# Attention steps in one hand-kept order: a second buffer for compressed scores, small work in other places of six steps, outputs split in mid-step, weights split later

## The chip, the cores and the metric

The kernel runs on one core of a Trainium2 chip. The metric is the device time of one execution in microseconds (us); of several executions the median is given. The engines are named as the profile names them: PE (TensorE, with its weight loads as PEld), DVE (VectorE), ACT (ScalarE), POOL (GpSimd) and SP (SyncE, which here only issues DMAs). Each engine works through its own instructions strictly in order; an instruction whose semaphore has not come holds up everything behind it on that engine.

## What is computed

Two decoder layers on one sequence of 512 tokens of width 1024: a convolution module with a feed-forward net, then native sparse attention with a feed-forward net. Only the attention matters here. Cut to that:

```python
def nsa_attention(h, positions, w_in, q_gain, k_gain, cmp_pos, cmp_w1, cmp_b1, cmp_w2, w_out):
    # 16 heads of 64, 4 key/value groups, three branches: compressed, selected, window
    proj = h @ w_in                       # q, 6 x k/v, gates
    ...
    s_c = einsum(q, k_cmp) * scale        # 31 compressed keys of one group
    p_c = masked_softmax(s_c, cmp_end <= t)
    o_c = einsum(p_c, v_cmp)
    ...                                   # all 8 blocks are within the top 16, so
    p_s = masked_softmax(einsum(q, k_s) * scale, tok <= t)     # causal over 512 keys
    o_s = einsum(p_s, v_s)
    p_w = masked_softmax(einsum(q, k_w) * scale, mask_w)       # a window of 512: causal too
    o_w = einsum(p_w, v_w)
    o = g[0] * o_c + g[1] * o_s + g[2] * o_w
    return o @ w_out
```

## The kernel before

Everything is kept transposed: features on the 128 partitions, the 512 tokens along the free axis. A matrix in fp32 is split into a high part (rounded to fp32r) and the rest, so a product is two or three matmuls; the splits are an ACT copy for the high part and a DVE subtraction for the low part.

Heads are worked two at a time. A *tile* `j` (0 to 7) holds two heads; a *pair* `p` (0 to 3) holds tiles `2p` and `2p+1`. A *unit* is one tile in one branch, selected (`br` 1) or window (`br` 2), so there are 16 units, in the order of `us`. The loop at the end of `nsa` runs steps `n` = 1 to 17: step `n` makes the scores of unit `n`, transposes the probabilities of unit `n-1` and multiplies them with the values; the last product of unit `n-2` falls at the head of the step. Unit 0's scores are made ahead of the loop.

In the loop the order on every engine is as the code is written (`fixed[0] = hold[0] = True`; `kept`, `pe` and `keep_in_program_order` mark the instructions). Outside the loop, and for DMA issues without such a mark, a planner with its own cost model sets the order. One step does this:

- `sc_(par, t)`: scores of 128 queries against up to 512 keys for one head (`L1746`, `L1747`: two matmuls into a PSUM tile `S`, of which there are three), then on DVE the mask and the row maximum (`L1749`, into `Pm`), then on ACT the exponential with its row sum (`L1750`).
- `weigh_(par, t)`: DVE reciprocal of two row sums (`L1760`), then POOL scales two blocks of `Pm` by it and by the gate (`L1764`).
- `flip_`: four PE transposes of `Pm` (`L1777`) into a PSUM tile `T`, copied out as `t` by ACT (`L1782`, tags `t2`, `t0`) or by DVE (`L1780`, tag `t1`).
- `values`: the products with the values into the PSUM tile `O` (`L1803`); for `br` 1 they begin with the compressed branch's product, `pch`, `pcl` with `vch`, `vcl` (`L1795` to `L1797`).
- `o_split`: when a tile's `O` is complete (at the head of steps 3, 5, ... 17), ACT copies the high part `oh` (`L1815`) and DVE subtracts for `ol` (`L1816`). It stands just ahead of slot d.
- four *slots* "a" to "d", at fixed places in the step, where `slot(z)` runs the small work that `q_pair` put into `work[n, z]`.

The small work of a pair is its query tiles and its compressed branch: `move` (four DMAs from SP, which make two stacked copies `q2` of a query tile; three buffers), `stack_hi` (the high part `St`, one copy on POOL `L1499` and one on ACT `L1501`), `stack_lo` (DVE subtraction on 64 partitions, `L1507`), `scores` (eight small matmuls into the PSUM tile `psc`, `L1513`), `masked` (DVE, `psc` into the SBUF tile `sc`, `L1518`; it reads and writes one half of `sc` for each tile of the pair), `top` (`L1528`), `minus` (`L1531`), `exps` (ACT, `L1534`), `valid` (POOL, `L1537`), `sums` (four DVE instructions, `L1543` to `L1549`), `weighed` (POOL, `L1552`), `trans` (four PE transposes of `sc` into the PSUM tile `pct`, `L1557`) and `parts` (ACT `pch` `L1564`, DVE `pcl` `L1565`). Pair 0 does this ahead of the loop, but for `trans` and `parts` (`qp0[4]`, step 1). `sc` has one buffer, so the first `masked` of a pair waits for the `trans` of the pair before.

PSUM has eight banks: three for `S`, two for `O`, and three (tag `p2`) that `T`, `psc` and `pct` share. A tile of tag `p2` gets the bank that the planner expects to be free first.

`W_AT` names the steps at whose end the first two weight tiles of the output projection are split (`w_hi` on ACT, `L219`; `w_lo` on DVE, `L228`); the projection (`proj_tile`, `L279` to `L281`) follows the loop.

Of the kernel before, what the change touches and what calls it, by code (L numbers as in the profile page):

```python
# [19 lines left out]
P = 128  # L20
T = 512
# [99 lines left out]
def trunk(ctx: ExitStack, tc: tile.TileContext, A, out):  # L121
    nc = tc.nc
# [1076 lines left out]
    def nsa(acc, gnext):  # L1199
# [3 lines left out]
        for i in range(2):  # L1203
            t = rp.tile([P, T], F32, name=f"tab{i}")
# [13 lines left out]
        def consts(p):  # L1218
            z = qk.tile([P, T], F32, tag="q2", name="cn", bufs=Q2B)
            nc.sync.dma_start(z[:, :256], A["cn"][:, N_VM:N_VM + 256])  # L1220
            ez = [qk.tile([64, T], F32, tag=t, name=nm("cne"), bufs=b) for t, b in (("q2", Q2B), ("sc", 1))]
            for i in range(2):
                nc.sync.dma_start(ez[i][:, :384], A["cn"][:64, N_E + 384 * i:N_E + 384 * i + 384])
            sel = p.tile([P, 76], F32, name="sel")
            nc.sync.dma_start(sel, A["cn"][:, N_SEL:N_E])
            nc.sync.dma_start(mask[:, 384:], A["cn"][:, N_MASK:N_MASK + 128])
            er = p.tile([P, 6, P], F32R, name="er")
            nc.gpsimd.memset(er[64:].bitcast(F32), 0.0)

# [245 lines left out]
        def kept(z):  # L1475
            return tc.keep_in_program_order(z) if fixed[0] else z

        def q_pair(p):

            a = p // 2  # L1480
            sc = qk.tile([P, 4, 2, 64], F32, tag="sc", name=nm("sc"), bufs=1)

            def move(jj):
                q = oT[2 * p + jj]
                box["q2", jj] = []
                for par in range(2):
                    hs = slice(par * 64, par * 64 + 64)
                    q2 = qk.tile([P, T], F32, tag="q2", name=nm("q2"), bufs=Q2B)
                    for half in range(2):
                        nc.sync.dma_start(q2[half * 64:half * 64 + 64], q[hs])  # L1490
                    box["q2", jj].append(q2)

            def stack_hi(jj):
                S2 = qk.tile([P, 1088], F32R, tag="S", name=nm("St"), bufs=3)
                for par in range(2):
                    q2 = box["q2", jj][par]
                    S = S2[:, par * T:par * T + T]
                    if p > 0 and par in STK_P:
                        kept(nc.gpsimd.tensor_copy(S, q2))  # L1499
                    else:  # L1500
                        kept(nc.scalar.activation(S, q2, AF.Copy))  # L1501
                    qst[2 * p + jj, par] = S

            def stack_lo(jj, par):
                ls = slice(64 - par * 64, 128 - par * 64)
                S, q2 = qst[2 * p + jj, par], box["q2", jj][par]
                kept(nc.vector.tensor_tensor(S[ls], q2[ls], S[ls], ALU.subtract))  # L1507
# [9 lines left out]
            def masked(jj):  # L1517
                kept(nc.vector.scalar_tensor_tensor(  # L1518
                    sc[:, :, jj, :], box["psc", jj], -1.0,
                    cc[:, C_CADD:C_CADD + 256].rearrange("p (t n) -> p t n", t=4), ALU.mult, ALU.add))  # L1520
# [33 lines left out]
            def trans():  # L1554
                pt = box["pct"] = p2.tile([P, T], F32, tag="p2", name=nm("pct"))
                for t in range(4):
                    tc.keep_in_program_order(nc.tensor.transpose(  # L1557
                        pt[:, t * P:(t + 1) * P], sc[:, t].rearrange("p j n -> p (j n)"), ident))

            def parts():  # L1560
                pt = box["pct"]
                ph = q3[1].tile([P, T], F32R, tag="pch", name=nm("pch"))
                pl = q3[1].tile([P, T], F32R, tag="pcl", name=nm("pcl"))
                kept(nc.scalar.activation(ph, pt, AF.Copy))  # L1564
                kept(nc.vector.tensor_tensor(pl, pt, ph, ALU.subtract))  # L1565
                pcT[p] = (ph, pl)
# [6 lines left out]
            if p == 0:  # L1573
                return [lambda: (move(0), scores(0), masked(0)), lambda: (both(0), scores(1), masked(1)),
                        lambda: (move(1), top(), minus(), exps()), lambda: (both(1), valid(), sums(), weighed()),
                        lambda: (trans(), parts())]
            n = max(1, 4 * p - 4)
            jobs = {
                (n, "a"): [lambda: move(0)],
                (n, "c"): [lambda: scores(0)],  # L1580
                (n, "d"): [lambda: masked(0), lambda: stack_hi(0)],
                (n + 1, "a"): [lambda: stack_lo(0, 0)],
                (n + 1, "c"): [lambda: scores(1)],
                (n + 1, "d"): [lambda: masked(1), lambda: stack_lo(0, 1), lambda: move(1)],
                (n + 2, "a"): [top],
                (n + 2, "d"): [minus, exps, lambda: stack_hi(1)],
                (n + 3, "a"): [valid, lambda: stack_lo(1, 0)],
                (n + 3, "d"): [sums, weighed],
                (n + 4, "a"): [lambda: stack_lo(1, 1), trans],
                (n + 4, "b"): [parts],  # L1590
            }
            for z, fs in jobs.items():
                work.setdefault(z, []).extend(fs)

# [77 lines left out]
        qp0 = []  # L1672
# [111 lines left out]
        ob = {}  # L1784
# [22 lines left out]

        split_o = []

        def o_split():  # L1810
            while split_o:
                o = ob[split_o.pop()]
                h_ = op.tile([P, T], F32R, tag=f"o{len(oh)}", name=nm("oh"))
                l_ = oha.tile([P, T], F32R, name=nm("ol"))
                kept(nc.scalar.activation(h_, o, AF.Copy))  # L1815
                kept(nc.vector.tensor_tensor(l_, o, h_, ALU.subtract))  # L1816
                oh.append(h_)
                ol.append(l_)

        us = [(j, br) for j in range(8) for br in (1, 2)]  # L1820
# [23 lines left out]
        for n in range(1, N + 2):  # L1844
            S = n < N
            F = n <= N
            if S:
                start(n)

            def sc_(par, *ts):  # L1850
                if S:
                    for t in ts:
                        score(U[n][par], t)

            def weigh_(par, t):
# [12 lines left out]
            flip_("t2", nc.scalar, (0, 2), (1, 2))
            if n > 1:
                values(U.pop(n - 2), (0,))  # L1870
            slot("a")
            weigh_(0, 2)
            sc_(0, 1, 0)
            slot("b")
            flip_("t1", nc.vector, (0, 1), (0, 3))
            sc_(1, 3)
            weigh_(0, 0)
            flip_("t1", nc.vector, (1, 1), (1, 3))
            sc_(1, 2)
            slot("c")  # L1880
            if n == 1:
                qp0[4]()
            flip_("t0", nc.scalar, (0, 0))
            sc_(1, 1, 0)
            weigh_(1, 2)
            flip_("t0", nc.scalar, (1, 0))
            o_split()
            slot("d")
            weigh_(1, 0)
            if n in W_AT:  # L1890
                w_hi(state["next"] + W_AT.index(n))
                w_lo(state["next"] + W_AT.index(n))
            if F:
                values(U[n - 1], (3, 2, 1))
        assert not work, work
        o_split()
        fixed[0] = hold[0] = False
        sx.close()
        ax.close()
# [179 lines left out]
```

## Time and profile before

| | |
|---|---|
| median of 3 runs | 1237.39 us (1235.42 to 1237.41) |
| the profiled execution | 1237.64 us, of which the span from first to last instruction is 1235.9 us |
| mean granted TensorE clock | 0.996 |
| PE busy over the span | 97% |
| steps 1 to 15 of the loop | 688.56 to 835.97 us: 147.41 us |
| step 16 and 17, to the first matmul of the output projection | 835.97 to 842.46 us: 6.49 us |

A step is counted here from its first score matmul (`L1746` with 512 columns, head 0) to that of the next. A row of the view by windows gives a stretch, its length, the busy time of PE, PEld, DVE, ACT and POOL in it with the number of instructions, the clock that TensorE was granted (1.00 is full), the busy share of the DMA engines and their rate. A row of the timeline gives the start, the length, the engine, the line, the operation, the tiles it writes and reads, its shape, and in brackets how long the engine had been idle and what ended that. A row of the view of waits gives who waited for whom, the sum, how often, and the longest.

### The profile page before, as it was taken

The page shows a single profiled execution, that of the slowest core. Times are in us where ns is not written, and L with a number is a line of the kernel's source. Part 1 is how long each engine was busy: PE and PEld are TensorE (multiplying, and loading weights), DVE is VectorE, ACT ScalarE, POOL GpSimd, SP SyncE. Part 2 cuts the span into 40 slices and gives each one's busy share as a digit, 9 for nine tenths or more (in the row PEclk, how much of TensorE's full clock was granted, in tenths as well). Part 3 has the DMA queues.
Part 4 walks back from the last instruction along what each step waited for, and adds up shares of the span by engine and source line. Part 5 has one row for each costly group of instructions (what it writes and reads, how often), then busy time and mean ns, then how long its engine had stood idle before and what let it go on. Part 6 is the DMA issues. An engine that isn't in the chain of part 4 may idle for free.

```text
span 1235.9 us, 22090 instructions
## 1 busy us (share of the span) xinstructions
PE 1199.9 (97%) x8519; PEld 1042.9 (84%) x8519; DVE 900.8 (73%) x1722; ACT 604.2 (49%) x1116; POOL 245.3 (20%) x349
## 2 busy tenths in 40 slices
PE   9999999999999999999998989989999999999998
PEld 6788688799999989887777766667778999998998
DVE  6996598877777576866697767763597777766775
ACT  5221464455555444543444667773354555554443
POOL 2011002011111102202332556652000111110120
PEclk9999999999999999999999999999999999999999
DMA  8748628277777667554265011015323877774882
GB/s 303 266 129 300 173 85 238 86 180 185 183 186 176 156 192 157 110 182 114 61 146 154 18 27 27 9 35 154 103 85 114 194 183 187 186 175 120 226 164 92
DMA packets 88378, 181.11 MB, mean 147 GB/s; under 512 B 36816, under 2 KB 38480, under 8 KB 86736
## 3 DMA queue, kind: packets, MB, share of 16 engines
q1 hardware_dynamic: 66816, 109.99, 29.2%
q0 software_dynamic: 21456, 69.71, 24.7%
q8 instruction: 67, 1.10, 0.4%
q14 instruction: 39, 0.32, 0.1%
HBM read 165.60 MB, written 5.80 MB: 139 GB/s over the span
## 4 chain that ended last, share of the span: by engine, by line
PE 79%; DVE 9%; ACT 4%; issue 3%; SPq 2%; DMA 2%; POOL 1%; DVEq 0%; ACTq 0%; POOLq 0%
PE st L915 27%; PE st L1105 10%; PE pp L279 7%; PE pp L281 7%; PE pp L280 7%; PE st L281 2%; PE st L280 2%; PE st L279 2%; PE cpe L540 2%; PE pv L1639 2%; PE O L1803 2%; ACT Pm L1750 2%; DVE Pm L1749 1%; PE T L1777 1%; DVE wl L228 1%
## 5 line engine op out<-in xcount | busy, mean ns | idle before, releaser
L219 ACT ACTIVATE wh<-wr 128x1024 fp32r<-128x1024 f32 (+4 forms) x150 | 152.9, 1019 | 201.8 <-PE pp L280 67.7
L228 DVE TENSOR_TENSOR wl<-wr,wh 128x1024 fp32r<-128x1024 f32 (+4 forms) x150 | 180.8, 1205 | 47.8 <-ACT wh L219 47.6
L915 PE MATMUL st<-bh,sl 128*128 128x256 f32 x680 | 192.6, 283 | 1.1 <-DVE sl L899 1.1
L915 PE MATMUL st<-bh,sh 128*128 128x256 f32 x680 | 192.7, 283 | 0.0
L915 PE MATMUL st<-bl,sh 128*128 128x256 f32 x680 | 192.1, 282 | 0.0
L279 PE MATMUL pp<-hh,wh 128*128 128x512 f32 x400 | 159.6, 402 | 2.2 <-ACT wh L219 2.1
L281 PE MATMUL pp<-hh,wl 128*128 128x512 f32 x400 | 157.9, 398 | 1.4 <-DVE wl L228 1.4
L280 PE MATMUL pp<-hl,wh 128*128 128x512 f32 x400 | 158.4, 397 | 0.0
L915 PEld LDWEIGHTS st<-bh,sl 128*128 128x128 f32 x680 | 130.2, 192 | 1.5 <-DVE sl L899 1.5
L915 PEld LDWEIGHTS st<-bl,sh 128*128 128x128 f32 x680 | 130.6, 192 | 0.1
L915 PEld LDWEIGHTS st<-bh,sh 128*128 128x128 f32 x680 | 130.0, 191 | 0.1
L899 DVE TENSOR_TENSOR sl<-S,sh 128x512 fp32r<-128x512 f32 x136 | 87.9, 688 | 51.7 <-ACT sh L898 51.7
L1764 POOL TENSOR_SCALAR Pm<-Pm,sm,gates 128x512 f32<-128x512 f32 (+3 forms) x128 | 81.4, 648 | 70.6 <-DVE sm L1760 63.5
L279 PEld LDWEIGHTS pp<-hh,wh 128*128 128x128 f32 x400 | 75.8, 190 | 23.2 <-ACT wh L219 4.6
L1750 ACT ACTIVATE Pm<-Pm,mx 128x512 f32<-128x512 f32 (+3 forms) x128 | 71.1, 556 | 49.3 <-DVE mx L1749 36.6
L281 PEld LDWEIGHTS pp<-hh,wl 128*128 128x128 f32 x400 | 75.5, 189 | 20.3 <-DVE wl L228 3.1
L280 PEld LDWEIGHTS pp<-hl,wh 128*128 128x128 f32 x400 | 75.8, 190 | 18.0 <-issue 1.1
L1105 PE MATMUL st<-oz,soh 128*128 128x256 f32 x448 | 79.6, 280 | 0.0
L898 ACT ACTIVATE sh<-S 128x512 fp32r<-128x512 f32 x136 | 77.6, 620 | 0.0
L915 PE MATMUL st<-bl,wh 128*128 128x256 f32 x272 | 76.2, 280 | 0.0
L915 PE MATMUL st<-bh,wl 128*128 128x256 f32 x272 | 76.1, 280 | 0.0
L915 PE MATMUL st<-bh,wh 128*128 128x256 f32 x272 | 76.1, 280 | 0.0
(308 smaller groups left out, 2778.8 us busy)
## 6 DMA issues: line engine op xcount, KB each, us to landing
S<-fw_x POOLq DMA_DIRECT2D x68, 512.0 KB, 5.9
wr<-fw_in SPq DMA_DIRECT2D x46, 512.0 KB
So<-fw_q POOLq DMA_DIRECT2D x38, 448.0 KB, 5.8
bd<-bands POOLq DMA_DIRECT2D x12, 1280.0 KB, 11.9
wr<-fw_q SPq DMA_DIRECT2D x24, 448.0 KB
r<-fw_x SPq DMA_DIRECT2D x34, 256.0 KB
wr<-fw_p SPq DMA_DIRECT2D x16, 512.0 KB
wr<-cw_in SPq DMA_DIRECT2D x14, 512.0 KB
```

The lines of the kernel that those rows point to most:

```text
L219: parted(after(nc.scalar.activation(hi[:, :cols], raws[i][:, :cols], AF.Copy), pin.get(AF)))
L228: parted(after(nc.vector.tensor_tensor(lo[:, :cols], raws[i][:, :cols], hi[:, :cols], ALU.subtract), pin.get(ALU)))
L279: held(nc.tensor.matmul(ps, wh, xh, start=first, stop=False))
L280: held(nc.tensor.matmul(ps, wh, xl, start=False, stop=False))
L281: held(nc.tensor.matmul(ps, wl, xh, start=False, stop=last))
L540: last["conv"] = nc.tensor.matmul(ps[e * 64:e * 64 + 16 * m, g, :], w, f[:, g0 + g, 4 - s:68 - s], start=s == 0, stop=s == 4)
L898: pe(nc.scalar.activation(h_[:, c], z, AF.Copy))
L899: pe(nc.vector.tensor_tensor(l_[:, c], z, h_[:, c], ALU.subtract))
L915: pe(nc.tensor.matmul(ps[:, :H], p_[:, k], m_[c][:, t], start=first and c == 0 and q == 0, stop=last and c == 3 and q == 2, skip_group_che ...
L1105: pe(nc.tensor.matmul(ps, a[:, c], b[:, t], start=p in (1, 4) and i == 0 and r == 0, stop=i == NO - 1 and r == 2, skip_group_check=True))
L1750: kept(nc.scalar.activation(Pt, Pt, AF.Exp, bias=mx, scale=-1.0, accum_out=sm))
L1764: kept(nc.gpsimd.tensor_scalar(Pt, Pt, sm[:, k:k + 1], gates[:, t + k, br * 16 + h:br * 16 + h + 1], ALU.mult, ALU.mult))
```

## The change

`sc` gets a second buffer. The two weight tiles are split at the end of steps 14 and 16, not 13 and 14. `o_split` becomes `o_hi`, which stands at the head of slot b's work ahead of the `t1` flips, and `o_lo`, which stands after the last score ahead of slot c. Pair 0's `trans` moves to the front of slot a in step 1, and its `parts` to the place ahead of slot c. Pairs 1 to 3 get new places, spread over six steps:

| small work | pair 1, before | pair 1, after | pairs 2, 3 (`n` = 4, 8), before | pairs 2, 3, after |
|---|---|---|---|---|
| `move(0)` | 1a | 1a | n, a | n+1, d |
| `scores`, `masked` of both tiles | 1c, 1d, 2c, 2d | the same | n and n+1, c and d | the same |
| `stack_hi(0)`, `stack_lo(0, ·)` | 1d; 2a, 2d | the same | n, d; n+1, a and d | n+2, a; n+2, d and n+3, a |
| `top`; `minus`, `exps` | 3a; 3d | 3a | n+2, a; d | n+2, c; d |
| `move(1)` | 2d | 3d | n+1, d | n+3, b |
| `valid`; `sums`, `weighed` | 4a; 4d | 3b; 3d | n+3, a; d | the same |
| `trans`; `parts` | 5a; 5b | 4a; 4c | n+4, a; b | n+4, a; c |
| `stack_hi(1)`, `stack_lo(1, ·)` | 3d; 4a, 5a | 4a; 4d, 5a | n+2, d; n+3, a and n+4, a | n+4, a; n+4, d and n+5, a |

```diff
-W_AT = (13, 14)
+W_AT = (14, 16)
...
-            sc = qk.tile([P, 4, 2, 64], F32, tag="sc", name=nm("sc"), bufs=1)
+            sc = qk.tile([P, 4, 2, 64], F32, tag="sc", name=nm("sc"), bufs=2)
...
-            n = max(1, 4 * p - 4)
+            n = 4 * p - 4
             jobs = {
-                (n, "a"): [lambda: move(0)],
                 (n, "c"): [lambda: scores(0)],
-                (n, "d"): [lambda: masked(0), lambda: stack_hi(0)],
-                (n + 1, "a"): [lambda: stack_lo(0, 0)],
+                (n, "d"): [lambda: masked(0)],
                 (n + 1, "c"): [lambda: scores(1)],
-                (n + 1, "d"): [lambda: masked(1), lambda: stack_lo(0, 1), lambda: move(1)],
-                (n + 2, "a"): [top],
-                (n + 2, "d"): [minus, exps, lambda: stack_hi(1)],
-                (n + 3, "a"): [valid, lambda: stack_lo(1, 0)],
+                (n + 1, "d"): [lambda: masked(1), lambda: move(0)],
+                (n + 2, "a"): [lambda: stack_hi(0)],
+                (n + 2, "c"): [top],
+                (n + 2, "d"): [minus, exps, lambda: stack_lo(0, 0)],
+                (n + 3, "a"): [valid, lambda: stack_lo(0, 1)],
+                (n + 3, "b"): [lambda: move(1)],
                 (n + 3, "d"): [sums, weighed],
-                (n + 4, "a"): [lambda: stack_lo(1, 1), trans],
-                (n + 4, "b"): [parts],
+            } if p > 1 else {
+                (1, "a"): [lambda: move(0)],
+                (1, "c"): [lambda: scores(0)],
+                (1, "d"): [lambda: masked(0), lambda: stack_hi(0)],
+                (2, "a"): [lambda: stack_lo(0, 0)],
+                (2, "c"): [lambda: scores(1)],
+                (2, "d"): [lambda: masked(1), lambda: stack_lo(0, 1)],
+                (3, "a"): [top, minus, exps],
+                (3, "b"): [valid],
+                (3, "d"): [sums, weighed, lambda: move(1)],
             }
+            jobs.update({
+                (n + 4, "a"): [trans, lambda: stack_hi(1)],
+                (n + 4, "c"): [parts],
+                (n + 4, "d"): [lambda: stack_lo(1, 0)],
+                (n + 5, "a"): [lambda: stack_lo(1, 1)],
+            })
...
-        def o_split():
+        def o_hi():
             while split_o:
-                o = ob[split_o.pop()]
-                h_ = op.tile([P, T], F32R, tag=f"o{len(oh)}", name=nm("oh"))
+                j = split_o.pop()
+                h_ = op.tile([P, T], F32R, tag=f"o{j}", name=nm("oh"))
+                kept(nc.scalar.activation(h_, ob[j], AF.Copy))
+                oh.append(h_)
+
+        def o_lo():
+            if len(ol) < len(oh):
                 l_ = oha.tile([P, T], F32R, name=nm("ol"))
-                kept(nc.scalar.activation(h_, o, AF.Copy))
-                kept(nc.vector.tensor_tensor(l_, o, h_, ALU.subtract))
-                oh.append(h_)
+                kept(nc.vector.tensor_tensor(l_, ob[len(ol)], oh[-1], ALU.subtract))
                 ol.append(l_)
...
+            if n == 1:
+                qp0[4]()
             slot("a")
             weigh_(0, 2)
             sc_(0, 1, 0)
             slot("b")
+            o_hi()
             flip_("t1", nc.vector, (0, 1), (0, 3))
             sc_(1, 3)
             weigh_(0, 0)
             flip_("t1", nc.vector, (1, 1), (1, 3))
             sc_(1, 2)
+            o_lo()
+            if n == 1:
+                qp0[5]()
             slot("c")
-            if n == 1:
-                qp0[4]()
             flip_("t0", nc.scalar, (0, 0))
             sc_(1, 1, 0)
             weigh_(1, 2)
             flip_("t0", nc.scalar, (1, 0))
-            o_split()
             slot("d")
             weigh_(1, 0)
```

More of the change, by code (lines that the diff above doesn't have):

```diff
@@ L1220, in consts @@
             nc.sync.dma_start(z[:, :256], A["cn"][:, N_VM:N_VM + 256])
-            ez = [qk.tile([64, T], F32, tag=t, name=nm("cne"), bufs=b) for t, b in (("q2", Q2B), ("sc", 1))]
+            ez = [qk.tile([64, T], F32, tag=t, name=nm("cne"), bufs=b) for t, b in (("q2", Q2B), ("sc", 2))]
             for i in range(2):
@@ L1575, in q_pair @@
                         lambda: (move(1), top(), minus(), exps()), lambda: (both(1), valid(), sums(), weighed()),
-                        lambda: (trans(), parts())]
-            n = max(1, 4 * p - 4)
+                        trans, parts]
+            n = 4 * p - 4
             jobs = {
-                (n, "a"): [lambda: move(0)],
                 (n, "c"): [lambda: scores(0)],
-                (n, "d"): [lambda: masked(0), lambda: stack_hi(0)],
-                (n + 1, "a"): [lambda: stack_lo(0, 0)],
+                (n, "d"): [lambda: masked(0)],
                 (n + 1, "c"): [lambda: scores(1)],
-                (n + 1, "d"): [lambda: masked(1), lambda: stack_lo(0, 1), lambda: move(1)],
-                (n + 2, "a"): [top],
-                (n + 2, "d"): [minus, exps, lambda: stack_hi(1)],
-                (n + 3, "a"): [valid, lambda: stack_lo(1, 0)],
-                (n + 3, "d"): [sums, weighed],
-                (n + 4, "a"): [lambda: stack_lo(1, 1), trans],
-                (n + 4, "b"): [parts],
-            }
+                (n + 1, "d"): [lambda: masked(1), lambda: move(0)],
[4 more added lines that the diff above has]
+                (n + 3, "b"): [lambda: move(1)],
+                (n + 3, "d"): [sums, weighed],
+            } if p > 1 else {
[8 more added lines that the diff above has]
+                (3, "d"): [sums, weighed, lambda: move(1)],
+            }
+            jobs.update({
[4 more added lines that the diff above has]
+            })
             for z, fs in jobs.items():
@@ L1895, in nsa @@
         assert not work, work
-        o_split()
         fixed[0] = hold[0] = False
```

## The prediction

> **What bounds the kernel now.** I read the page's first lines, then the loop cut at its steps (the view by windows: steps 1 to 15, and last the drain), then PE's waits inside the loop, then the timeline at each long wait.
>
> ```profile
> span 1235.9 us, 22090 instructions
> core 0: us, PE busy (x) PEld busy (x) DVE busy (x) ACT busy (x) POOL busy (x), PEclk, DMA share, GB/s
> 688.56:699.61 11.05, 9.21 (x65) 6.95 (x63) 7.22 (x29) 8.34 (x24) 5.17 (x9) 1.00 0.00 0
> 699.61:708.06 8.45, 8.45 (x62) 6.31 (x60) 6.72 (x25) 6.00 (x19) 4.70 (x8) 1.00 0.15 33
> 708.06:716.37 8.31, 8.31 (x58) 5.89 (x56) 5.59 (x22) 6.11 (x20) 5.31 (x10) 1.00 0.15 34
> 716.37:726.37 10.00, 8.95 (x63) 6.41 (x61) 8.78 (x27) 7.27 (x21) 6.12 (x10) 1.00 0.12 26
> 726.37:741.42 15.05, 11.77 (x70) 8.29 (x68) 8.85 (x31) 8.64 (x26) 7.26 (x12) 0.89 0.16 36
> 741.42:749.02 7.60, 7.60 (x54) 5.43 (x52) 6.92 (x26) 5.14 (x15) 3.76 (x7) 1.00 0.17 37
> 749.02:757.64 8.62, 8.53 (x57) 5.87 (x55) 6.07 (x24) 7.79 (x26) 7.92 (x12) 1.00 0.14 32
> 757.64:769.60 11.96, 9.21 (x67) 6.67 (x65) 8.41 (x30) 6.81 (x21) 5.88 (x9) 1.00 0.10 23
> 769.60:778.75 9.15, 9.15 (x66) 6.77 (x64) 5.85 (x23) 8.13 (x25) 6.74 (x11) 1.00 0.14 30
> 778.75:786.93 8.18, 8.04 (x55) 5.52 (x53) 7.43 (x27) 4.93 (x16) 3.54 (x7) 1.00 0.00 0
> 786.93:795.78 8.85, 8.50 (x57) 5.86 (x55) 6.35 (x24) 8.02 (x26) 8.14 (x12) 1.00 0.01 2
> 795.78:807.30 11.52, 8.52 (x58) 5.83 (x56) 8.10 (x29) 6.37 (x19) 5.42 (x9) 1.00 0.00 1
> 807.30:815.88 8.58, 8.54 (x58) 5.87 (x56) 5.17 (x22) 7.21 (x24) 5.77 (x10) 1.00 0.01 3
> 815.88:825.35 9.47, 8.41 (x55) 5.59 (x53) 6.86 (x24) 6.72 (x18) 4.90 (x8) 1.00 0.18 55
> 825.35:835.97 10.62, 9.32 (x57) 6.03 (x55) 6.25 (x23) 7.88 (x24) 5.49 (x10) 1.00 0.16 51
> 835.97:842.46 6.49, 6.24 (x42) 3.30 (x41) 2.15 (x4) 2.83 (x7) 3.22 (x6) 1.00 0.30 89
> ```
>
> Good steps are PE's own work: steps 2, 3, 6 and 9 have PE busy for their whole length. Step 6, 7.60 us, is the bare step; step 3 has the compressed product besides (8.31, so 0.7); step 2 has eight `psc` matmuls besides (8.45, so 0.85). Steps 1, 4, 5, 8, 12, 14 and 15 are longer because PE stood still. Those are what this change can win. It is PE's waits that name the causes:
>
> ```profile
> PE S L1746 <- DVE mx L1749: 4.5, 6, 1.1
> PE pct L1557 <- POOL sc L1552: 3.5, 2, 1.7
> PE psc L1513 <- DVE pcl L1565: 2.6, 2, 1.6
> PE T L1777 <- ACT t L1782: 1.8, 2, 1.1
> PE T L1777 <- DVE pcl L1565: 1.0, 1, 1.0
> ```
>
> Now the timeline where these begin: DVE, then PE, POOL and ACT.
>
> ```profile
> 700.49 0.69 DVE L1749 CUSTOM_DVE_ANT_0 Pm<-S,mask 128x512 f32<-128x512 f32 x1 [1.92 <-POOL Pm L1764]
> 708.84 0.69 DVE L1749 CUSTOM_DVE_ANT_0 Pm<-S,mask 128x512 f32<-128x512 f32 x1 [0.82 <-PE S L1747]
> 717.27 0.69 DVE L1816 TENSOR_TENSOR ol<-O,oh 128x512 fp32r<-128x512 f32 x1 [2.16 <-ACT oh L1815]
> 719.74 1.86 DVE L1507 TENSOR_TENSOR St<-q,St 64x512 fp32r<-64x512 f32 x1
> 729.59 0.42 DVE L1518 SCALAR_TENSOR_TENSOR sc<-psc,cc 128x256 f32<-128x256 f32 x1 [2.36 <-PE pct L1557]
> 758.65 0.69 DVE L1816 TENSOR_TENSOR ol<-O,oh 128x512 fp32r<-128x512 f32 x1 [2.16 <-ACT oh L1815]
> 764.89 0.69 DVE L1565 TENSOR_TENSOR pcl<-pct,pch 128x512 fp32r<-128x512 f32 x1 [1.33 <-ACT pch L1564]
> 817.74 1.24 DVE L228 TENSOR_TENSOR wl<-wr,wh 128x1024 fp32r<-128x1024 f32 x1 [0.19 <-ACT wh L219]
> 696.92 0.52 PE L1777 MATMUL T<-cc,Pm 128*128 128x128 f32 x3 [1.15 <-ACT t L1782]
> 761.90 0.66 PE L1557 MATMUL pct<-cc,sc 128*128 128x128 f32 x4 [1.72 <-POOL sc L1552]
> 788.57 0.44 PE L1777 MATMUL T<-cc,Pm 128*128 128x128 f32 x2 [0.35 <-POOL Pm L1764]
> 719.76 1.29 POOL L1537 TENSOR_TENSOR sc<-sc,cc 128x512 f32<-128x512 f32 x1
> 704.68 0.72 ACT L1750 ACTIVATE Pm<-Pm,mx 128x512 f32<-128x512 f32 x1 [0.49 <-DVE sm L1760]
> 842.60 0.60 ACT L1815 ACTIVATE oh<-O 128x512 fp32r<-128x512 f32 x1 [1.63 <-PE O L1803]
> 843.23 0.69 DVE L1816 TENSOR_TENSOR ol<-O,oh 128x512 fp32r<-128x512 f32 x1 [3.15 <-ACT oh L1815]
> 721.63 1.10 SPq L1490 DMA_DIRECT2D q<-qraw  x2
> ```
>
> And one row of the view of the tile `sc` (least, middle and greatest duration in ns); `minus` and the first of `sums` are as long.
>
> ```profile
> L1528 DVE TENSOR_REDUCE cm<-sc x4: 674/678/681, 680.6 to 781.5; 128x16 f32<-128x512 f32 x4
> ```
>
> The pattern: DVE comes to a small instruction whose input is late (`ol` on `oh`, `masked` on pair 1's `trans`, `pcl` on `pch`), stands 1.3 to 2.4 us, and the row maxima queued behind it come late; PE, three `S` banks ahead, then stops. The granted clock fell to 0.89 in step 5, after its three gaps: 15.05 × 0.11 = 1.66 us of that step.
>
> **The change part by part.** PE's own work by step, from the differences above and about 0.45 for `trans` (0.66 in the row at 761.90, whose last 0.2 runs on beside the next matmul): bare 7.6; odd steps 8.3; plus 0.85 in steps 1, 2, 4, 5, 8, 9; plus 0.45 in steps 4, 8, 12 (before 5, 8, 12).
>
> *The second buffer of `sc`.* It takes away the 2.36 us before 729.59. But `trans` of pair 1 now stands in 4a, ahead of pair 2's `masked` in 4d, so one buffer would no longer be waited for either: price and gain by itself 0. It adds 2 KB per partition and no instruction.
>
> *Pair 1 a step earlier, step 5.* `top`, `minus`, `exps` in 3a put two DVE instructions of 0.68 and one ACT instruction into step 3. DVE waits for ACT there anyway, but `recip` comes about 0.3 late; step 3 has DVE busy 5.59 of 8.31, so 0.05: 8.35. Step 5 keeps `stack_lo(1,1)` and `masked`, gets `ol` in mid-step, and loses `trans`, `parts`, two subtractions and the wait. PE's work is 8.3 + 0.85 = 9.15; step 9 ran such a load in 9.15. I take 9.4 for POOL's lateness: 15.05 − 9.4 = 5.65 won, 1.66 of it clock.
>
> *Steps 4 and 8, with `trans` in a and `parts` in c.* PE's work is 7.6 + 0.85 + 0.45 = 8.9. In slot c `psc` and `pct` are both held, so the two `t0` flips share the third bank, and the second waits for ACT's copy of the first, which ACT makes behind `pch`. Step 1 has just this arrangement, and its row at 696.92 gives the price: 1.15. DVE's 1.33 before `pcl` stays, later in the step. So about 8.9 + 1.15 + 0.25 = 10.3 (step 4 10.2): step 4 loses 0.2, step 8 wins 1.65. Bounds: −1.15 (the bank is free) to +2.15 more (below).
>
> *`trans` in time, steps 8 and 12.* It waited 1.72 for `weighed`, which waited for `sums`, which stood behind `ol` (758.65). DVE had been free from 756.49 on; with `ol` (0.69) done there or earlier, `sums` and with it `weighed` come about 2.1 sooner, at 759.8, and PE came to `trans` at 760.18. In step 12 no `psc` is made, so no bank is short: work 8.05, taken 8.4, won 3.1.
>
> *`oh` and `ol` in mid-step.* ACT is idle 0.49 before the `L1750` at 704.68 where `oh` (0.60) goes now: 0.1 late at most. `ol` (0.69) goes ahead of the maxima of the last two scores; PE needs these one step later. Behind `ol` no longer stand `sums`, a reciprocal and the next step's maxima. If that cover were gone it would cost 0.69 in seven steps, 4.8.
>
> *Steps 6, 7, 10, 11.* `stack_hi(0)` in a: 0.6 on ACT and on POOL, which have 5.14 and 3.76 of 7.60 busy. `top` moves to c (0.68 ahead of two maxima). New in d: `minus` and `stack_lo(0,0)` back to back on DVE just when POOL is to scale the two blocks that the next step's first flip reads. Already with `minus` alone that flip waited 0.35 (788.57). I take 0.8: steps 7 and 11 become 9.1, a loss of 0.5 and 0.25. Step 6 7.7 (+0.1), step 10 7.8 (−0.4).
>
> *Steps 9 and 13.* `stack_lo(1,1)` replaces `stack_lo(0,0)`: 9.15 to 9.4 and 8.58 to 8.6, since they inherit DVE's lag: +0.27.
>
> *The moves.* Four DMA issues each, on SP, 0.55 us an issue; only weight loads stand in that queue here. SP starts them when a `q2` buffer is free (721.63, right after the subtraction that ended at 721.60), wherever they are written. Each lands at least a step before its `stack_hi` in the new places: 0.
>
> *Weights.* `wh` and `wl` (1.24 for the latter) go from the ends of steps 13 and 14 to 14 and 16. Step 14 no longer starts with DVE behind `wl`: 9.47 to 7.9. Step 15 still does: 10.62 to 10.4. In the drain ACT idles 1.63 and DVE 3.15 before the last `oh` and `ol`, which covers the second split; the drain goes from 6.49 to 6.2 as `ol` no longer delays step 15's last scaling. The freed buffers let two weight loads start later, but they are used two projections on: 0.
>
> *Step 1* has the same order on ACT and DVE as before: 11.0. Sum: step 4 +0.2, 5 −5.65, 6 +0.1, 7 +0.5, 8 −1.65, 9 and 13 +0.27, 10 −0.4, 11 +0.25, 12 −3.1, 14 −1.55, 15 −0.2, drain −0.3, steps 1 and 3 0: −11.5 us. The profiled execution took 1237.64 us, 0.25 above the median of 1237.39; 1237.6 − 11.5 = 1226.1, so 1226.0 against the median. Outside the loop the planner orders; the change gives it nothing to reorder there that I can see. I take 0; the ends are the clock's loss in step 5, 1.66 either way.
>
> The clock's return is counted in. [...]
>
> **The rivals.** *All waits go.* If the third bank and POOL are in time too, steps 2 to 14 come to PE's own work, 108.6 in place of the 114.7 that I sum: 1220. Against it: step 1's 1.15 under the same bank arrangement.
>
> *DVE and POOL in each other's way.* The subtraction at 719.74 took 1.86, not 0.69, and ended 0.55 after `valid`, which had begun with it. The new 7a and 11a put `valid` and a subtraction side by side, with POOL on time, and 6d and 10d add the pair of DVE instructions beside POOL's scaling. Price: 2 × (1.17 + 0.68) = 3.7, so 1229.7. [...]
>
> *`psc` waits for `parts`.* If the planner gives `psc` the bank of `pct`, PE stands from the last score to the end of `pcl`: exponential, 0.58 copy, 0.69 subtraction and the hand-overs, 3.3 in place of 1.15 in steps 4 and 8: 4.3, and 1.66 if the clock falls: 1230 to 1232. For it: 2.6 us of such waits now. Against: `t1`'s copy now comes before `pcl` on DVE.
>
> *The other side: DVE's round sets the pace.* In step 2 DVE's round from first maximum to first maximum is 708.84 − 700.49 = 8.35, as long as the step. If each small instruction put into the middle lengthens it, steps 2 to 14 cost 13 × 8.35 = 108.6 plus 28 us (10 subtractions 6.9, three `top`, `minus`, `sums` 8.2, four `masked` 1.6, three `pcl` with waits 6.1, six `ol` 4.1, `wl` 1.2): 136.6 in place of 125.7, so 1248.5. It decides, at slower by 2.5 us, when 70% of them are exposed. Against it: step 2 hid two subtractions and a `masked`, 1.8 us, with PE busy throughout.
>
> **How the numbers follow.** The forecast, 1222 to 1229, gets 0.55. All waits go, 0.12. DVE against POOL, 0.12; `psc` behind `parts`, 0.06: all faster. Gains given back down to within 0.2% (2.5 us, about what three runs can tell here), by two of these with a lower clock outside the loop, 0.07. DVE's pace, 0.08. So faster 0.85, same 0.07, slower 0.08. From 1219 to 1234 leaves out the last two and half of the best case's lower end.
>
> **What would show it.** Right: step 5 near 9.4 at clock 1.00; no `DVE sc <- PE pct` wait; no 2.16 before `ol`; `pct <- POOL sc` gone in 8 and 12; step 14 below 8.2; a PE wait on ACT's `t` of about 1 us late in steps 4 and 8. Wrong: subtractions of over 1.5 us in 7a and 11a; `psc <- pcl` of 3 us; DVE's maxima ending PE's waits in most steps; or a stage outside 688 to 843 that changed length.

## The result, and the profile after

The changed kernel takes 1226.24 us (median of 4 runs, 1224.24 to 1228.15); beside it the kernel before took 1237.16 (4 runs). The ratio is 0.9915, 95% interval 0.9895 to 0.9934: 10.9 us won, against 11.4 forecast (1237.39 to 1226.0).

The profiled execution of the changed kernel took 1228.15 us, with a span of 1226.3. Against the span of 1235.9 before, 9.6 us are gone: 8.5 in the loop (688.56 to 842.46, 153.90 us, before; 687.35 to 832.74, 145.39 us, after), 1.2 ahead of it, and behind it nothing (393.4 and 393.6). The view by windows, cut at the first score of each step as before (the last row is the drain, steps 16 and 17 up to the first matmul of the output projection):

```profile
core 0: us, PE busy (x) PEld busy (x) DVE busy (x) ACT busy (x) POOL busy (x), PEclk, DMA share, GB/s
687.35:698.39 11.04, 9.12 (x65) 6.90 (x63) 7.21 (x29) 8.33 (x24) 5.15 (x9) 1.00 0.00 0
698.39:706.85 8.46, 8.46 (x63) 6.32 (x61) 6.71 (x25) 6.01 (x19) 4.67 (x8) 1.00 0.15 33
706.85:715.15 8.30, 8.30 (x58) 5.88 (x56) 7.46 (x26) 6.74 (x22) 6.08 (x10) 1.00 0.15 34
715.15:725.50 10.35, 9.21 (x67) 6.79 (x65) 7.62 (x29) 7.76 (x23) 6.78 (x11) 1.00 0.01 2
725.50:734.65 9.15, 9.15 (x66) 6.77 (x64) 6.58 (x25) 6.73 (x20) 5.73 (x11) 1.00 0.26 57
734.65:742.25 7.60, 7.60 (x54) 5.42 (x52) 5.72 (x23) 5.50 (x16) 3.71 (x8) 1.00 0.00 0
742.25:751.63 9.38, 8.53 (x58) 5.87 (x56) 8.95 (x28) 8.01 (x26) 7.93 (x11) 1.00 0.27 59
751.63:761.98 10.35, 9.21 (x67) 6.79 (x65) 7.58 (x29) 7.64 (x22) 6.66 (x10) 1.00 0.01 2
761.98:771.13 9.15, 9.15 (x66) 6.77 (x64) 6.58 (x25) 6.73 (x20) 5.72 (x11) 1.00 0.26 57
771.13:778.73 7.60, 7.60 (x54) 5.42 (x52) 5.72 (x23) 5.50 (x16) 3.71 (x8) 1.00 0.00 0
778.73:788.11 9.38, 8.53 (x57) 5.88 (x55) 8.94 (x28) 8.01 (x26) 7.92 (x11) 1.00 0.13 30
788.11:796.29 8.18, 8.18 (x59) 5.83 (x57) 5.50 (x21) 6.14 (x17) 5.57 (x9) 1.00 0.00 0
796.29:808.07 11.78, 10.33 (x58) 6.61 (x56) 8.04 (x32) 7.84 (x26) 6.44 (x10) 0.86 0.01 3
808.07:815.67 7.60, 7.60 (x54) 5.42 (x52) 5.04 (x22) 5.53 (x16) 4.35 (x8) 1.00 0.00 0
815.67:826.23 10.56, 9.32 (x59) 6.23 (x57) 6.76 (x24) 8.26 (x26) 5.12 (x9) 1.00 0.15 51
826.23:832.74 6.51, 6.01 (x40) 3.11 (x39) 2.02 (x4) 3.19 (x5) 3.82 (x8) 1.00 0.50 180
```

Read length against PE's busy time: steps 2, 3, 5, 6, 9, 10, 12 and 14 are now PE's own work, with no gap. Steps 1, 4, 7, 8, 11, 13 and 15 still have one. Their causes, from PE's waits inside the loop (total, times, longest):

```profile
PE T L1791 <- ACT t L1796: 4.0, 4, 1.1
PE T L1791 <- POOL Pm L1778: 3.6, 4, 1.5
PE S L1760 <- DVE mx L1763: 1.0, 1, 1.0
```

Of the five causes shown for before, three are gone (`pct` on `sc`, 3.5; `psc` on `pcl`, 2.6; `T` on `pcl`, 1.0); the maxima fell from 4.5 in six waits to 1.0 in one. The wait for ACT's copy grew from 1.8 to 4.0, and POOL's scaling, 0.6 before, has become the second cause. The first is the shortage of a bank, seen here in step 4 (timeline of ACT, then PE): ACT makes `pch`, then the copy of the first `t0` flip, and only then can PE write the second one.

```profile
722.29 0.58 ACT L1564 ACTIVATE pch<-pct 128x512 fp32r<-128x512 f32 x1
722.76 0.59 ACT L1796 ACTIVATE t<-T 128x512 f32<-128x512 f32 x1
...
723.50 0.63 PE L1791 MATMUL T<-cc,Pm 128*128 128x128 f32 x4 [1.14 <-ACT t L1796]
```

The second cause, in the timeline of step 13 (DVE, POOL, PE), then three rows from steps 2 and 7 to compare:

```profile
795.86 0.69 DVE L1565 TENSOR_TENSOR pcl<-pct,pch 128x512 fp32r<-128x512 f32 x1 [1.25 <-ACT pch L1564]
797.02 0.16 DVE L1774 RECIPROCAL sm<-sm 128x2 f32<-128x2 f32 x1
797.21 0.69 DVE L1507 TENSOR_TENSOR St<-q,St 64x512 fp32r<-64x512 f32 x1
797.38 1.16 POOL L1778 TENSOR_SCALAR Pm<-Pm,sm,gates 128x512 f32<-128x512 f32 x1 [2.75 <-DVE sm L1774]
799.24 0.44 PE L1791 MATMUL T<-cc,Pm 128*128 128x128 f32 x2 [1.45 <-POOL Pm L1778]
...
701.79 0.77 POOL L1778 TENSOR_SCALAR Pm<-Pm,sm,gates 128x512 f32<-128x512 f32 x1 [2.24 <-DVE sm L1774]
742.67 1.16 DVE L1507 TENSOR_TENSOR St<-q,St 64x512 fp32r<-64x512 f32 x1
745.29 1.72 POOL L1537 TENSOR_TENSOR sc<-sc,cc 128x512 f32<-128x512 f32 x1
```

Step 12 ends with PE on time and DVE late: DVE stood 1.25 for `pch`, so the reciprocal at 797.02, which POOL's scaling waits for, comes into step 13. The scaling then runs beside a subtraction and takes 1.16 in place of the 0.77 at 701.79. PE's first flip stands 1.45. Right behind it the granted clock is 0.86 over the step, which costs 11.78 × 0.14 = 1.6 us.

### The profile page after: what moved, and what is told of

It is laid out like the page before. It is cut to its first block, busy times and chain, and to the rows that moved or that the text cites. A ratio compares the mean times of both kernels' runs of the same rounds, so it can differ in the third digit from the quotient of the medians.

```text
span 1226.3 us, 22079 instructions
## 1 busy us (share of the span) xinstructions
PE 1195.1 (97%) x8519; PEld 1039.0 (85%) x8519; DVE 901.8 (74%) x1722; ACT 603.5 (49%) x1116; POOL 244.4 (20%) x349
## 4 chain that ended last, share of the span: by engine, by line
PE 80%; DVE 9%; issue 3%; ACT 3%; DMA 2%; SPq 2%; POOL 1%; DVEq 0%; POOLq 0%; ACTq 0%
PE st L915 28%; PE st L1105 10%; PE pp L281 7%; PE pp L279 7%; PE pp L280 7%; PE st L281 2%; PE st L280 2%; PE st L279 2%; PE cpe L540 2%; PE O L1817 2%; PE T L1791 2%; PE pv L1653 2%; DVE wl L228 1%; PE S L1760 1%; DVE Pm L1763 1%
```

## The experiments

All ran in rounds against the kernel before, whose medians were 1236.64 us in the rounds of experiments 1 to 4, 1236.82 in those of 5 to 8 and 1235.64 in those of 9 to 11; each ratio is made within its rounds. "Loop" is the time from the first score of step 1 to the first matmul of the output projection in the profiled execution. Ratios have their 95% interval. Where *at full clock* is said of whole runs, it is an estimate: the run's span times its mean granted clock, which each run lists, averaged over the runs of a kernel. The clock is listed to a thousandth, about 1.2 us of a run.

| kernel | median us | ratio to before | loop us |
|---|---|---|---|
| before, profiled as above | 1237.16 | 1 | 153.90 (1.7 of it lower clock) |
| changed kernel | 1226.24 | 0.9915 [0.9895, 0.9934] | 145.39 (1.6 of it lower clock) |
| 1 before, two buffers | 1233.57 | 0.9976 [0.9959, 0.9992] | 151.88 |
| 2 before, pair 1 moved | 1235.25 | 0.9992 [0.9977, 1.0008] | 152.27 |
| 3 changed, one buffer | 1226.73 | 0.9919 [0.9897, 0.9940] | 143.77 |
| 4 changed, outputs split late | 1232.32 | 0.9966 [0.9953, 0.9979] | 149.88 |
| 5 changed, `psc` later | 1228.22 | 0.9937 [0.9910, 0.9964] | 146.10 (about 1.7 lower clock) |
| 6 changed, `pch` earlier | 1221.37 | 0.9867 [0.9839, 0.9895] | 139.15 |
| 7 changed, subtractions apart | 1226.89 | 0.9920 [0.9896, 0.9945] | 145.01 |
| 8 both of 6 and 7 | 1222.13 | 0.9882 [0.9857, 0.9908] | 140.33 |
| 9 changed, weights early | 1230.34 | 0.9942 [0.9920, 0.9964] | 145.52 |
| 10 = 6, and pairs 2, 3 spread like pair 1 | 1222.67 | 0.9888 [0.9870, 0.9907] | 138.76 |
| 11 = 10, and weights split elsewhere | 1221.21 | 0.9871 [0.9850, 0.9893] | 136.79 |

**1. The second buffer alone**, in the kernel before (the constants' tile that shares the tag `sc` gets the same number).

```diff
-            sc = qk.tile([P, 4, 2, 64], F32, tag="sc", name=nm("sc"), bufs=1)
+            sc = qk.tile([P, 4, 2, 64], F32, tag="sc", name=nm("sc"), bufs=2)
```

> The kernel before, with the second buffer of sc and nothing else. Theory (the buffer takes away only the 2.36 us that DVE stood ahead of 729.59; parts in 5b still hold DVE and PE): step 5 falls from 15.05 to 11.5 to 13 us, the PE wait psc <- pcl stays at about 1.5 us, the time falls by 2 to 4 us, to about 1234. Rival (the buffer carries what step 5 won): step 5 near 9.3 and 1231 to 1232 us. Rival (it moves nothing, since DVE then waits for pch in its place): step 5 over 14 us, 1236 to 1238.

Steps 5 and 6 by windows, and one of PE's waits:

```profile
727.96:739.55 11.59, 9.89 (x70) 7.14 (x68) 8.49 (x29) 7.92 (x25) 7.93 (x12) 1.00 0.21 47
739.55:748.40 8.85, 8.41 (x55) 5.60 (x53) 7.43 (x27) 5.61 (x17) 3.67 (x8) 1.00 0.13 30
...
PE psc L1513 <- DVE pcl L1565: 2.7, 2, 1.7
```

Step 5 falls from 15.05 to 11.59, but 1.66 of that is the clock, which stayed at 1.00 here, and step 6 gives 1.25 back (8.85 for 7.60). The wait of `psc` for `pcl` stays. Against 152.2 us of loop at full clock, the buffer's own gain is 0.3. The expected 2 to 4 us came out (1236.64 to 1233.57), but not for the expected reason: over whole runs at full clock 1.4 of the 3.1 us are left (1231.5 to 1230.1), and the others are clock. Whether the buffer spares the clock isn't shown, and the 1.1 beyond the loop's 0.3 stay open.

**2. Pair 1's new places alone**, in the kernel before, with one buffer.

```diff
+            if p == 1:
+                jobs = {
...
+                    (3, "a"): [top, minus, exps],
+                    (3, "b"): [valid],
+                    (3, "d"): [sums, weighed, lambda: move(1)],
+                    (4, "a"): [trans, lambda: stack_hi(1)],
+                    (4, "c"): [parts],
...
```

> The kernel before, with one buffer, and the new places for pair 1 alone (its trans in 4a and parts in 4c). Theory (the order is enough, the buffer is not needed): no DVE wait for trans before masked, step 5 near 9.3 at full clock, step 4 about 10.3, time lower by 5 to 6 us, about 1231.5. Rival (the buffer is needed): DVE still waits 1 us or more before masked of pair 2, and step 4 or 5 stays over 11 us.

```profile
715.94:728.14 12.20, 9.31 (x66) 6.80 (x64) 8.65 (x31) 8.25 (x24) 6.49 (x10) 1.00 0.00 1
728.14:737.91 9.77, 9.41 (x65) 6.79 (x63) 6.30 (x23) 6.56 (x20) 6.45 (x11) 1.00 0.37 81
...
PE pct L1557 <- POOL sc L1552: 5.2, 3, 1.8
```

Step 5 came out close to what was expected (9.77 for 9.3; before, 13.39 at full clock), step 4 not: 12.20 for 10.00, because `trans` of pair 1, now in 4a, waits for `weighed` behind the late `ol`, as pairs 2 and 3 always did (5.2 us in three waits for 3.5 in two). Step 5 wins 3.6 at full clock, step 4 gives back 2.2 of them, and steps 6 and 7 another 1.5 (8.83 and 8.85 for 7.60 and 8.62). So the expected 5 to 6 us did not come: alone, the move wins nothing.

**3. The changed kernel with one buffer** (`bufs=1` in both places).

> The changed kernel with one buffer of sc. Theory: every masked already comes after the trans of the pair before in program order, so nothing waits: within 0.2% of the changed kernel, 1224 to 1228.5, the same steps. Rival (the buffer is needed): over 1230, with a DVE wait before masked.

Step 13 and the loop:

```profile
797.53:807.71 10.18, 8.72 (x57) 5.79 (x56) 7.96 (x32) 7.84 (x26) 6.43 (x10) 1.00 0.01 3
...
688.62:832.39 143.77, 134.65 (x907) 95.19 (x905) 106.32 (x386) 107.94 (x313) 89.65 (x138) 1.00 0.11 29
```

Every other step agrees with the changed kernel's to 0.02 us, and step 13 differs by the clock alone: 10.18 at 1.00 for 11.78 at 0.86. So the second buffer is worth nothing in the new order, as predicted, and 143.8 is the changed kernel's loop at full clock.

**4. The outputs split late again**, in the changed kernel.

```diff
             slot("b")
-            o_hi()
...
-            o_lo()
             if n == 1:
                 qp0[5]()
...
             flip_("t0", nc.scalar, (1, 0))
+            o_hi()
+            o_lo()
             slot("d")
```

> The changed kernel with oh and ol back at their old place, ahead of slot d. Theory (ol behind a late oh made sums, weighed and so trans late): PE waits for weighed ahead of trans in steps 4, 8 and 12, 1.5 to 1.9 us each, and DVE stands 2.16 us before ol again; the time rises by 4 to 6 us over the changed kernel, to 1230 to 1232. Rival (the new places of the small work alone do it): within 2 us of the changed kernel.

```profile
689.10:838.98 149.88, 135.50 (x906) 95.33 (x905) 105.46 (x386) 108.03 (x313) 88.85 (x137) 1.00 0.10 25
...
PE pct L1557 <- POOL sc L1552: 5.0, 3, 1.8
```

The loop is 6.1 longer at full clock (149.88 against 143.77), and the three waits of `trans` for `weighed` are back, 5.0 us. Of the parts taken out here it carries most, but the rest without it still wins 2.3 (152.2 to 149.88). Without it steps 4, 8 and 12 take 12.20, 12.08 and 9.89 in place of 10.35, 10.35 and 8.18.

**5. `psc` a slot later**, to leave a bank free in slot c (pairs 2 and 3).

```diff
-                (n, "c"): [lambda: scores(0)],
-                (n, "d"): [lambda: masked(0)],
+                (n, "d"): [lambda: scores(0)],
+                (n + 1, "a"): [lambda: masked(0)],
```

> The changed kernel with scores(0) of pairs 2 and 3 in slot d (4d, 8d) and masked(0) in the next slot a. Theory (the 1.14 us wait of the second t0 flip in steps 4 and 8 is a shortage of p2 banks: psc and pct both held): the PE wait T <- ACT t goes from steps 4 and 8, and as in step 13, which follows a step without psc, the first flip of steps 5 and 9 then waits for POOL's scaling, about 0.6 us each; net 1 us won, 1225 against 1226.2. Rival (no shortage, ACT's copies are just late there): the 1.14 us stay. Rival (nothing comes back): 2.3 us won.

```profile
722.08 0.66 PE L1513 MATMUL psc<-kcb,qraw 128*128 128x64 f32 x4 [1.46 <-ACT t L1796]
```

None of the three expectations was met. The flip no longer waits in steps 4 and 8, but `psc` does, 1.46 for the same copy: in both orders it was the third user of the three banks that waited (the flip 1.14, `psc` 1.46). Step 8 is 10.74 for 10.35.

**6. `pch` early**, so that `pct` gives its bank back sooner. `parts` is cut in two: `part_hi`, ACT's copy into `pch`, goes to slot b, ahead of the copies of slot c; `part_lo`, DVE's subtraction, stays in c. For pair 0 the two stand ahead of slot b and ahead of slot c of step 1.

```diff
-                (n + 4, "c"): [parts],
+                (n + 4, "b"): [part_hi],
+                (n + 4, "c"): [part_lo],
...
+            if n == 1:
+                qp0[5]()
...
```

> The changed kernel with parts taken apart: pch on ACT in slot b (pair 0: ahead of slot b), pcl on DVE where parts stood. Theory (DVE stands 1.26 us before pcl because pch is queued behind the last exponential, and all scaling behind it comes late): no DVE wait before pcl; the PE wait T <- ACT t in steps 1, 4 and 8 falls from 1.14 to 0.6 or less, and T <- POOL Pm in step 13 from 1.45 to 0.4 or less; 2 to 3.5 us won, 1222.5 to 1224.5. Rival (ACT then makes the next exponentials late, and the wait comes back as S <- DVE mx): within 1 us of the changed kernel.

The loop, step 13 and two of PE's waits, then the end of step 4 on DVE, ACT and PE:

```profile
693.88:833.03 139.15, 134.47 (x906) 95.27 (x905) 106.27 (x386) 107.50 (x313) 89.92 (x138) 1.00 0.12 31
799.51:808.35 8.84, 8.52 (x58) 5.87 (x56) 6.84 (x26) 7.25 (x24) 6.17 (x10) 1.00 0.02 4
...
PE T L1794 <- POOL Pm L1781: 2.5, 4, 0.9
PE T L1794 <- ACT t L1799: 0.6, 1, 0.6
...
726.99 0.69 DVE L1567 TENSOR_TENSOR pcl<-pct,pch 128x512 fp32r<-128x512 f32 x1
727.72 0.58 ACT L1799 ACTIVATE t<-T 128x512 f32<-128x512 f32 x1
727.82 0.63 PE L1794 MATMUL T<-cc,Pm 128*128 128x128 f32 x4
```

All three waits of 1.14 are gone (steps 1, 4 and 8: 9.94, 9.24, 9.24 for 11.04, 10.35, 10.35), and step 13 shrinks from 10.18 to 8.84, because DVE no longer stands 1.25 for `pch` at the end of step 12. Together 3.3 + 1.3 = 4.6, and the loop is 4.6 shorter than experiment 3's. It could also be that ACT's copy merely comes earlier, with `pch` no longer ahead of it; the three rows of step 4 decide that. The second `t0` flip begins at 727.82, when `pcl` has ended (727.68) and ACT's copy of the first flip is still running (to 728.30), and `psc` is still held (DVE reads it at 729.06); so it is written into the bank that `pct` gave back. Experiment 6 is the smallest edit here that beats both kernels: its interval ends where the changed kernel's begins.

**7. The subtractions of `stack_lo` apart**, away from `minus` and from POOL's scaling.

```diff
-                (n + 2, "d"): [minus, exps, lambda: stack_lo(0, 0)],
+                (n + 2, "b"): [lambda: stack_lo(0, 0)],
+                (n + 2, "d"): [minus, exps],
...
-                (n + 4, "d"): [lambda: stack_lo(1, 0)],
-                (n + 5, "a"): [lambda: stack_lo(1, 1)],
+                (n + 5, "a"): [lambda: stack_lo(1, 0)],
+                (n + 5, "c"): [lambda: stack_lo(1, 1)],
```

> The changed kernel with the subtractions St taken away from POOL's scaling at the end of steps 6, 10 and 4, 8, 12: stack_lo(0,0) of pairs 2 and 3 in slot b of the same step, stack_lo(1,0) of all pairs in the next slot a, stack_lo(1,1) in that step's slot c. Theory (DVE work with two SBUF inputs and POOL's scaling hold each other up): POOL's scaling of 128x512 takes 0.77 rather than 1.07 to 1.16 there, the PE wait T <- POOL falls from 0.85 to about 0.35 in steps 7 and 11 and from 1.45 to about 0.9 in step 13; 1.5 us won, about 1224.7. Rival (the scaling is late because its reciprocal is): the three waits stay within 0.2 us.

```profile
737.90 0.38 PE L1761 MATMUL S<-kst,St 128*128 128x256 f32 x1 [0.66 <-DVE mx L1764]
```

Half right. POOL's wait falls in steps 7 and 11 (0.85 to 0.61 and 0.63) and 13 (1.45 to 1.06). But the subtraction in slot b holds the maxima, and PE waits 0.66 for them in steps 6 and 10, which had no gap. Loop 145.01: 1.2 longer than 143.8.

**8. Experiments 6 and 7 together.**

> The changed kernel with both: pch in slot b and the subtractions apart. Theory: what the two win adds up, and step 13's wait goes whole: 4 to 5 us less than the changed kernel, about 1221.5, a loop of about 139 us from its first score to the output projection. Rival (the waits replace one another): no better than the better of the two.

Loop 140.33, 1.2 longer than 6 alone: the gaps of 0.66 stay, and step 13, whose wait is now gone (8.42), gains 0.4. What the two win doesn't add up.

**9. The weights split at the end of steps 13 and 14**, as before the change.

```diff
-W_AT = (14, 16)
+W_AT = (13, 14)
```

> The changed kernel with the two weight tiles split at the ends of steps 13 and 14 again. Theory (a step that starts with DVE behind wl loses 1 to 2 us of PE; step 15 loses that either way, and step 16 covers its own): a wait S <- DVE mx of about 0.8 comes in step 14, which grows from 7.6 to about 9.3; 1.5 us lost, about 1227.7. Rival (the drain had to pay for the split at step 16): within 0.5 us, the drain shorter by what step 14 loses.

Step 14, and DVE in it:

```profile
809.61:818.65 9.04, 8.40 (x54) 5.59 (x52) 6.26 (x23) 6.23 (x17) 4.13 (x8) 1.00 0.16 58
...
810.98 1.29 DVE L228 TENSOR_TENSOR wl<-wr,wh 128x1024 fp32r<-128x1024 f32 x1 [1.26 <-ACT wh L219]
```

Step 14 is 9.04 for 7.60, and step 15 with the drain 17.35 for experiment 3's 17.07: 1.75 in the loop. DVE stands 1.26 for `wh` and works 1.29, with step 14's maxima behind it. The median moved by 4; over whole runs at full clock it is 1.9 (1223.2 to 1225.1), about what the loop shows.

**10 and 11. Two more steps from 6.** In 10 pairs 2 and 3 get pair 1's spread: `stack_lo(0, 0)` in `n+2`c, `stack_lo(0, 1)` in `n+2`d, `top`, `minus`, `exps` in `n+3`a, `valid` in `n+3`b. In 11 besides, `wh` stands at the ends of steps 13 and 14 and `wl` in slot a of the next step.

> The kernel with pch in slot b, and besides it pairs 2 and 3 as pair 1 has them: top, minus, exps in slot a of steps 7 and 11, valid in b, and the subtractions of the first tile in 6c, 6d, 10c, 10d. Theory (the wait T <- POOL in steps 7 and 11 comes of two DVE instructions back to back in 6d and 10d, and the late place in slot a costs nothing, as in step 3): the wait falls from 0.86 to 0.35 or less, steps 7 and 11 from 9.38 to 8.3 to 8.9; 1 to 2 us less than with pch in slot b alone, about 1220. Rival (steps 7 and 11 are full: DVE busy 8.95 of 9.38): PE waits for DVE's maxima there instead, no gain.

> The kernel of the run beside it (pch in slot b, top, minus, exps in slot a), and the weights split in two parts: the ACT copy at the ends of steps 13 and 14, the DVE subtraction in slot a of steps 14 and 15, where DVE stands about 1 us for ACT. Theory: the waits S <- DVE mx of step 15 (0.99 and two of 0.14) go or fall below 0.4, step 15 from 10.56 to about 9.3; 1 us less than the run beside it, about 1219. Rival (1.24 us do not fit into a 1.06 us gap): the wait comes in both steps, no gain.

The loop of 11 (that of 10 is in the table), then one of PE's waits, which reads the same in both:

```profile
691.12:827.91 136.79, 133.75 (x906) 95.14 (x905) 105.82 (x386) 107.59 (x313) 88.28 (x138) 1.00 0.13 35
...
PE T L1794 <- POOL Pm L1781: 2.1, 4, 0.7
```

10 takes 0.2 from each of steps 7 and 11 (9.38 to 9.19), less than the 1 to 2 us expected. 11 takes the wait for the maxima out of step 15 and shortens step 15 with the drain from 17.08 to 15.10. Of the 136.79 only 3.0 are PE standing. The medians don't show it: 1222.67 and 1221.21 beside experiment 6's 1221.37, with overlapping intervals. Over whole runs at full clock 6, 10 and 11 average 1218.5, 1217.6 and 1216.0, and the kernel before in their rounds 1231.9, 1231.1 and 1231.1; so 11 is ahead of 6 by 1.7 to 2.5, as its loop is by 2.4. In the medians the clock hides it.

## Why the prediction was right, and where not

| step | 4 | 5 | 6 | 7 | 8 | 9 | 10 | 11 | 12 | 13 | 14 | 15 | drain |
|---|---|---|---|---|---|---|---|---|---|---|---|---|---|
| predicted | 10.2 | 9.4 | 7.7 | 9.1 | 10.3 | 9.4 | 7.8 | 9.1 | 8.4 | 8.6 | 7.9 | 10.4 | 6.2 |
| measured | 10.35 | 9.15 | 7.60 | 9.38 | 10.35 | 9.15 | 7.60 | 9.38 | 8.18 | 11.78 | 7.60 | 10.56 | 6.51 |

- **Size.** Twelve of the thirteen terms are within 0.31 us. The loop was to win 11.5 and won 8.5 in the profiled execution, where the two loops' low-clock stretches cancel (1.7 and 1.6). With both clocks full, 11.5 − 1.66 = 9.8 was forecast and 152.2 − 143.8 = 8.4 came. That the median's 10.9 lies so near the forecast is luck: about 2.5 of it is the clock and not the loop. In 52 runs of the kernel before (those beside the experiments) the mean granted clock averages 0.997, in the four of the changed kernel 0.999; over whole runs at full clock they average 1231.5 and 1223.2, 8.3 apart. That the change itself spares the clock isn't shown: with one buffer, experiment 3, the same order averages 0.9975.
- **The signs.** All that were named for "right" are in the trace. Of those for "wrong" one came, a stage outside the loop that changed length: the stretch ahead of it is 1.2 shorter. Its instructions have the same order on every engine; before, the clock was 0.50 there for 6.83 us (from 675.35), after, for 3.41 us (from 612.03), and the difference costs 1.7 us.
- **Step 13 is the term that failed.** "`stack_lo(1,1)` replaces `stack_lo(0,0)`: 9.15 to 9.4 and 8.58 to 8.6" is so in step 9 alone; in step 13 no subtraction stood before. It also overlooked that `stack_lo(1,0)` comes in at 12d, beside the same POOL scaling, and that DVE comes out of step 12 late because of the 1.25 for `pch`, which the text had itself put at 1.33. Price: 10.18 at full clock for the 8.6, 1.45 of it waiting, which is about all that the loop lacks at full clock; and in this execution 1.6 of clock. Experiment 6 removes the wait for `pch`, and 1.34 of the step goes with it.
- **The bank shortage** in steps 4 and 8 was read off step 1 (1.15) and measured 1.14 and 1.14. Experiment 6 shows that it was avoidable, and that `pct`'s bank was the one missing.
- **The second buffer** was priced at 0: experiment 3 has 143.77 with one.
- **The outputs in mid-step** carried steps 8 and 12, as argued: experiment 4 loses 6.1 without it, and the 2.16 before `ol` is gone. Experiment 2 shows it from the other side: pair 1's earlier places, the largest term of the sum (5.65), do shorten step 5, but with `ol` late step 4 loses 2.2 to them, a price that the text saw for steps 8 and 12 alone.
- **Steps 5 and 9** were put 0.25 too high: POOL in step 5 and DVE in step 9 were in time.
- **The weights** were to win 2.05 in steps 14, 15 and the drain; undoing them costs 1.75.
- **DVE and POOL in each other's way**, the rival put at 0.12, happened in its two places, smaller: the subtraction took 1.16 and 0.85, not 1.86, the scaling 1.06 for 0.77 (1.16 in step 13), and `valid` 1.72 for the 1.29 of before. The steps it was to lengthen became 9.38, 0.28 above the forecast. Beside other work of DVE the same instructions kept their length: the scaling took 0.77 beside the maxima (701.79) and beside the first of `sums` (787.32), `valid` 1.29 beside the maxima and a copy (711.75). The lengthened ones ran beside `minus` or a `stack_lo`, which read two SBUF tiles each; that this is the reason is an inference from these rows.
- **DVE's pace**, the rival on the other side, did not come: PE waits for maxima once, 1.0, in step 15.
- **The clock.** It came back in step 5, as counted in (1.00 for 0.89), and fell in step 13 instead (0.86); with the same order it stayed full in experiment 3 (1.00 over the loop), so the fall doesn't come of the order alone.

## What to carry to other kernels

Where an engine works in the order of the code, as here (DVE stood 1.25 for `pch`, the reciprocal and POOL's scaling behind it came late, and PE stood 1.45), a small instruction that waits for another engine should be put where its input is already there; its own 0.7 us matter less than what stands behind it, and moves of this kind depend on one another: pair 1's alone won nothing in the loop (experiment 2), all but the output split 2.3 (experiment 4), all of them 8.4. With three banks shared in rotation, moving a user shifted the wait to another one (experiment 5, 1.46 for 1.14); releasing a bank sooner removed it (experiment 6, three waits of 1.14). Judge an edit of a few us by its own stage in the trace: most steps here repeat to 0.03 us from execution to execution, while the medians move by several us with the clock, so a run's time is best read beside its granted clock.

## What the runs showed of the hardware

**The clock fell in the loop after 3.41 us in which PE was busy for more than half.** Of the 13 profiled executions three have a mean granted clock of 1.000, the other ten 0.994 to 0.999: there the clock fell inside the kernel. In the two kernels' own traces it fell to 0.50, for 3.41 us (before at 736.79; after at 612.03 and 799.76) or twice that (before at 675.35), and the starts lie 61.44 us apart before and 187.73 after, which is 18 and 55 times 3.413. Three falls lie in the loop, two of them in these traces and one in experiment 5; PE was busy for 1.83 (before), 1.97 and 1.95 of the 3.41 us ahead of them, and the longest single waits of PE shortly before were 1.6, 1.45 and 1.46 us. The rows show the 3.41 us before a fall and the fall, in the changed kernel; then the same in experiment 5, around step 4's wait of 1.46; and, in the same experiment, the two stretches around step 8's wait of 1.46, with no fall:

```profile
796.34:799.76 3.42, 1.97 (x12) 1.17 (x12) 3.34 (x13) 2.42 (x8) 2.38 (x3) 1.00 0.01 2
799.76:803.17 3.41, 3.41 (x13) 1.81 (x11) 0.91 (x6) 1.41 (x5) 2.27 (x4) 0.50 0.03 5
...
719.59:723.00 3.41, 1.95 (x16) 1.55 (x14) 2.12 (x10) 2.54 (x7) 0.75 (x2) 1.00 0.02 5
723.00:726.42 3.42, 3.42 (x15) 1.74 (x15) 0.78 (x2) 1.10 (x5) 2.77 (x4) 0.50 0.35 77
757.13:760.54 3.41, 1.95 (x16) 1.51 (x14) 2.15 (x7) 2.49 (x6) 0.98 (x2) 1.00 0.01 2
760.54:763.95 3.41, 3.41 (x25) 2.48 (x26) 1.82 (x9) 1.47 (x5) 2.43 (x4) 1.00 0.23 50
```

In experiment 5 PE was busy for 1.95 of the 3.41 us both times, and the clock fell after only one of them (0.50 and 1.00), so PE's busy time alone doesn't decide. What else does stays open.

**Where the spread between runs arises.** In the 13 traces the time from the loop's end to the end of the span is 393.3 to 393.6 us, and the loop repeats; the loop's start varies from 684.37 (experiment 7, no fall ahead of it) to 693.88 (experiment 6, the clock at 0.87, 0.79 and 0.66 in the three stretches of 10 us from 660 on). The four traces without a fall there start at 684.37 to 688.13, so the clock explains only part of the spread. Over the 52 runs of the kernel before, taking the clock out (span times mean granted clock) halves the standard deviation, from 2.4 to 1.2 us.
